# Layer 2 of a hybrid decoder step: its first seven products read the un-normed residual, and LayerNorm is spread over the chunks

## The chip, the core and the metric

The kernel runs on one core of a Trainium2 chip. The metric is the device time of one execution in microseconds. One profiled execution gives the trace that is read below. TensorE multiplies matrices (a weight load, then a matmul that streams the columns of the other operand); VectorE, ScalarE and GpSimd do elementwise work; SyncE issues most transfers.

## The reference, cut to what matters

One inference step of a two-layer trunk over 320 tokens (256 of a prompt, 8 x 8 samples) with a model width of 2048. Each layer projects `x`, runs three branches (retention, pooling, windowed attention), merges them, projects back and norms the residual:

```python
h = x @ w_in                      # 2048 -> 13824, split in qa ka va ga ub gb qc kc vc gc ma mb mc
...                               # branches a, b, c
merged = sigmoid(ma) * ya + sigmoid(mb) * yb + sigmoid(mc) * yc
y = merged @ w_out
x_new = layer_norm(alpha * x + y, ln_g, ln_b)   # (z - mean) * rsqrt(var + eps) * g + b, over 2048
```

The input of layer 2 is the `layer_norm` of layer 1's residual. Everything is float32.

## The kernel before, in words

Activations lie transposed: 16 tiles of 128 features by T = 320 tokens, four tiles in one buffer. Each float32 operand is split in a rounded high part and the rest (`h`, `l` for weights; `xh`, `xl` for the layer's input), and each 128 x 128 weight block is multiplied in three matmuls: `xh` by `h`, `xh` by `l`, `xl` by `h`.

Weights come in chunks of CH = 8 blocks (24 matmuls), 297 chunks to a layer, in the order of `layer_groups`. Layer 2 begins with a group of four products side by side (`kc` 0, `vc` 0, `qc` 0, `qc` 1; 64 blocks, 8 chunks), then `qc` 2, `qc` 3, `kc` 1, `vc` 1 and so on, two chunks each. The last products of a layer are the 16 of `wo`, each of which leaves through `done_wo`.

The program order is written by hand in `run`, and each engine works its own queue in that order. In chunk c, at position 0, `split_h(c + 2)` copies the raw weights of a chunk to their high part (ScalarE, 1024 elements a partition); at position 4, `split_l(c + 2)` subtracts that from the raw weights (VectorE), and `load(c + 6)` issues a transfer on SyncE's queue. There are three buffers for `h` and three for `l`, so the split for chunk c + 2 can't start before TensorE is done with chunk c - 1: a split is up to two chunks ahead. At the end of a chunk `pump` runs: it takes CHUNK_US = 3.26 off each engine's ledger `busy` (floor -3.0), steps the `misc` generators, and then each of three lanes (attention, two of retention) once, if the ledger of ScalarE and VectorE is under LATE_US = 1.0. The ledger is booked by `act`, `tt`, `stt`, `ts` as an instruction is issued: `tt` and `stt` book 0.15 + elements / 960 on VectorE, which is 1.22 for a weight split and 0.483 for 320 elements.

A product accumulates in PSUM: three buffers `d` (pool `psd`), five `p`. When its last matmul is issued, `done_<kind>` takes it out: `done_kc`, `done_vc`, `done_qc` copy it on ScalarE.

At the layer boundary: `done_wo(j)` adds product j to the residual z and to the running sums S and Q (of z and z squared). After j = 15 TensorE sums S and Q over features (`token_sums`), VectorE and ScalarE compute mean and inverse deviation (`norm`, first lines), TensorE spreads both over the partitions (`token_rows`), and `norm` norms the 16 tiles into new `xh`, `xl`. That part is skewed by hand:

```python
if k < 12: center(k + 4, nc.gpsimd)   # z - mean, on GpSimd
if k < 13: scaled(k + 3)              # times 1/deviation, VectorE
if k < 14: high(k + 2)                # ScalarE: times g plus b, then the copy to xh
if k:      low(k)                     # VectorE: the rest, xl
```

`need_x(k + 3)` steps it within the first group. No product of layer 2 starts before `xh` of its first tile is there.

Of the kernel before, what the change touches and what calls it, by code (L numbers as in the profile page):

```python
# [21 lines left out]
T = NP + NB * NT  # L22
PAST = 1024
# [17 lines left out]
def att_rows(t):  # L41

    p, g = divmod(t, 4)
    lo, hi = (2 * p) * 4 + g, (2 * p + 1) * 4 + g
    return np.concatenate([np.arange(lo * 64, lo * 64 + 64), np.arange(hi * 64, hi * 64 + 64)])

# [48 lines left out]
class Job:  # L95
    __slots__ = ("kind", "i", "ps", "left", "w")

    def __init__(self, kind, i):
        self.kind, self.i, self.ps, self.left = kind, i, None, n_k(kind)


class Step:
    def __init__(self, ctx, tc, io):
        self.tc, self.nc, self.io = tc, tc.nc, io
        pool = lambda n, b, **kw: ctx.enter_context(tc.tile_pool(name=n, bufs=b, **kw))
        self.cp = pool("const", 1)
        self.gp = pool("gran", 24)
        self.mp = pool("mid", 13)
        self.np = pool("mini", 6)
        self.sp = pool("small", 8)  # L110
        self.wp = pool("w", 4)
        self.hp = pool("wh", 3)
        self.lp = pool("wl", 3)
        self.pd = pool("psd", 3, space=bass.MemoryType.PSUM)
        self.pp = pool("psp", 5, space=bass.MemoryType.PSUM)
        self.raw, self.H, self.L = {}, {}, {}
        self.busy = {"a": 0.0, "v": 0.0, "p": 0.0}
        self.lanes = {"att": deque(), "ret0": deque(), "ret1": deque()}
        self.misc = []

# [161 lines left out]
    def pump(self):  # L282

        for e in self.busy:
            self.busy[e] = max(self.busy[e] - CHUNK_US, -SLACK_US)
        self.step_misc()
        for lane in self.lanes:
            if max(self.busy["a"], self.busy["v"]) < LATE_US:
                self.step(lane)
# [10 lines left out]
    def setup(self):  # L300
        nc, io = self.nc, self.io
        self.ident = self.const("ident", [128, 128])
        make_identity(nc, self.ident[:])
        self.ident_r = self.cp.tile([128, 128], F32R, tag="ident_r", name="ident_r")
        nc.vector.tensor_copy(out=self.ident_r, in_=self.ident)
        self.ones = self.const("ones", [128, 128])
        nc.vector.memset(self.ones, 1.0)
        self.ones_r = self.cp.tile([128, 128], F32R, tag="ones_r", name="ones_r")
        nc.vector.memset(self.ones_r[:].bitcast(F32), 1.0)
        yield  # L310
        self.rot = self.const("rot", [128, 2, T], io["c_rot"], nc.sync)
        self.sinkP = self.const("sinkP", [128, DEPTH, 16], io["sink_p"], nc.sync)
        self.sinkS = self.const("sinkS", [128, DEPTH, 4], io["sink_s"], nc.sync)
        self.nsinkP = self.const("nsinkP", [128, DEPTH, 16])
        self.nsinkS = self.const("nsinkS", [128, DEPTH, 4])
        yield
        yield
        self.ts(self.nsinkP, self.sinkP, -1.0)
        self.ts(self.nsinkS, self.sinkS, -1.0)
        self.dmask = self.const("dmask", [128, HA, 128], io["c_dmask"])  # L320
        self.qdec = self.const("qdec", [128, HA, 128], io["c_qdec"])
        self.maskS = self.const("maskS", [128, HA, 128], io["c_masks"])
        self.kdec = self.const("kdec", [128, HA], io["c_kdec"])
        self.kdecS = self.const("kdecS", [128, HA, NT], io["c_kdecs"])
        self.cnt = self.const("cnt", [128, 4, 16], io["c_cnt"])
        self.pscale = self.const("pscale", [128, DEPTH, 8], io["pool_scale"])
        self.lng = self.const("lng", [128, DEPTH, 16], io["ln_g"])
        self.lnb = self.const("lnb", [128, DEPTH, 16], io["ln_b"])
        self.bmask = self.const("bmask", [128, 4, 80], io["c_bmask"])
        self.flip = self.const("flip", [128, 2], io["c_flip"])  # L330
        yield
        self.biasS = self.const("biasS", [128, 4, 160], io["bias_s"])


    def run(self):
# [30 lines left out]
        for layer in range(DEPTH):  # L366
            if layer:
                self.begin_layer(layer)
            for grp in layer_groups():
                jobs = [Job(kind, i) for kind, i in grp]  # L370
                self.before(jobs[0].kind, jobs[0].i)
                for k in range(n_k(grp[0][0])):
                    if len(jobs) > 1:
                        self.need_x(min(k + 3, 15))
# [19 lines left out]
    def block(self, job, k, c, pos):  # L394
        if job.ps is None:
            if job.kind == "qc" and job.i == 1:
                job.ps = self.p([128, T])
            else:
                job.ps = self.pd.tile([128, T], F32, tag="d", name="d")
# [14 lines left out]
    def part(self, pair, k):  # L414
        return pair[0][k // 4][:, k % 4, :], pair[1][k // 4][:, k % 4, :]
# [7 lines left out]
    def rhs(self, job, k):  # L423
        kind = job.kind
        if kind in ("ya", "yb", "yc"):
            return self.part(self.gated[kind[1]], k)
# [7 lines left out]
    def begin_layer(self, l):  # L434
# [3 lines left out]
        self.x_gen = self.x_from_input() if l == 0 else self.norm(l - 1, zs, False)  # L438
# [13 lines left out]

    def x_from_input(self):
        self.x = ([], [])
        for k in range(16):
            if k % 4 == 0:
                self.x[0].append(self.g([128, 4, T], F32R, name=f"xh{k}"))
                self.x[1].append(self.g([128, 4, T], F32R, name=f"xl{k}"))
# [4 lines left out]
    def before(self, kind, i):  # L463
# [14 lines left out]
        if kind == "wo" and i == 0:  # L478
            self.z = [self.g([128, 4, T], name=f"z{n}") for n in range(4)]

# [245 lines left out]

    def done_kc(self, p, ps):
        nc, l = self.nc, self.l
        kv = self.g([128, 2, T], name="kv")
        self.copy(kv[:, 0, :], ps)  # L730
# [7 lines left out]
    def done_vc(self, p, ps):  # L738
        nc, l = self.nc, self.l
        kv = self.att[p]["kv"]  # L740
        self.copy(kv[:, 1, :], ps)
# [3 lines left out]
    def done_qc(self, t, ps):  # L745
        p, g = divmod(t, 4)
        self.copy(self.att[p]["q"][:, g, :], ps)
# [247 lines left out]
    def done_wo(self, j, ps):  # L995
# [10 lines left out]
        if j == 1:  # L1006
            self.drain("misc")
            for i in range(2):
                zi = self.z[0][:, i, :]
                self.tt(zi, zi, self.cen, ALU.subtract)  # L1010
            self.S = self.m([128, T], name="S")
# [6 lines left out]
        self.tt(self.Q, self.Q, sq, ALU.add)  # L1018
        if j < 15:
# [7 lines left out]
        if j == 15:  # L1027
            self.pS, self.pQ = self.token_sums(self.S), self.token_sums(self.Q)

# [8 lines left out]
    def norm(self, l, zs, final):  # L1038
        nc = self.nc
        st = self.s(16)  # L1040
        mu, ms, v, y, t = (st[:, 3 * i:3 * i + 3] for i in range(5))
        tile_of = lambda k: zs[k // 4][:, k % 4, :]
        M = self.m([128, T], name="M")
# [4 lines left out]
        def affine(k, out):  # L1048
            g, b = self.lng[:, l, k:k + 1], self.lnb[:, l, k:k + 1]
            self.act(out=out, in_=tile_of(k), func=AF.Identity, bias=b, scale=g)  # L1050

        def affine_v(k, out):
            self.ts(out, tile_of(k), self.lng[:, l, k:k + 1], self.lnb[:, l, k:k + 1])
# [5 lines left out]
        self.act(out=t, in_=v, func=AF.Sqrt)  # L1059
# [4 lines left out]
        if final:  # L1064
            return self.last(tile_of, center, affine, affine_v, pR)
        center(0)
        for k in range(1, 4):
            center(k, nc.gpsimd)
        self.x = ([], [])
        for k in range(4):  # L1070
            self.x[0].append(self.g([128, 4, T], F32R, name=f"xh{k}"))
            self.x[1].append(self.g([128, 4, T], F32R, name=f"xl{k}"))

        def scaled(k):
            self.tt(tile_of(k), tile_of(k), pR, ALU.mult)

        first = {}

        def high(k):
            h = self.part(self.x, k)[0]  # L1080
            if k < 2:
                affine(k, h)
                first[k] = self.m([128, T], name="x0")
                affine_v(k, first[k])
            else:
                affine(k, tile_of(k))
                self.copy(h, tile_of(k))

        def low(k):
            h, lo = self.part(self.x, k)  # L1090
            self.tt(lo, first.get(k, tile_of(k)), h.bitcast(F32), ALU.subtract)

        def rest():
            for k in range(2):
                scaled(k)
                high(k)
            low(0)
            scaled(2)
            for k in range(16):
                if k < 12:  # L1100
                    center(k + 4, nc.gpsimd)
                if k < 13:
                    scaled(k + 3)
                if k < 14:
                    high(k + 2)
                if k:
                    low(k)
                yield

        return rest()  # L1110

    def last(self, tile_of, center, affine, affine_v, pR):
        nc = self.nc
# [37 lines left out]
    def finish(self):  # L1151
        self.norm(DEPTH - 1, self.z, True)
# [141 lines left out]
```

## Time and profile before

| | |
|---|---|
| runs (us) | median 2295.2, lowest 2294.62 |
| the profiled execution | 2294.67, of which the profile's span is 2292.8 |
| mean granted TensorE clock | 0.995 |
| TensorE busy | 99% of the span |
| VectorE, ScalarE, GpSimd busy | 53%, 41%, 4% |
| layer boundary | about 1138 to 1150 us |

Times in rows are microseconds from the span's start unless marked ns. A row of the timeline gives start, length, engine, line, operation, output<-input and the idle time in front of it with what ended it. Matmuls are pipelined, so a row of 0.31 us does not mean a pace of 0.31: the pace is the distance between starts. The same holds, less strongly, for VectorE and ScalarE. Many lines are those of helpers: L176 is `act`, L183 `tt`, L187 `stt`, L197 `mm`.

### The profile page before, as it was taken

The page shows a single profiled execution, that of the slowest core. Times are in us where ns is not written, and L with a number is a line of the kernel's source. Part 1 is how long each engine was busy: PE and PEld are TensorE (multiplying, and loading weights), DVE is VectorE, ACT ScalarE, POOL GpSimd, SP SyncE. Part 2 cuts the span into 40 slices and gives each one's busy share as a digit, 9 for nine tenths or more (in the row PEclk, how much of TensorE's full clock was granted, in tenths as well). Part 3 has the DMA queues.
Part 4 walks back from the last instruction along what each step waited for, and adds up shares of the span by engine and source line. Part 5 has one row for each costly group of instructions (what it writes and reads, how often), then busy time and mean ns, then how long its engine had stood idle before and what let it go on. Part 6 is the DMA issues. An engine that isn't in the chain of part 4 may idle for free.

```text
span 2292.8 us, 37711 instructions
## 1 busy us (share of the span) xinstructions
PE 2265.2 (99%) x15660; PEld 2213.3 (97%) x15660; DVE 1207.3 (53%) x1861; ACT 944.2 (41%) x1534; POOL 99.4 (4%) x155
## 2 busy tenths in 40 slices
PE   8999999999999999999999999999999999999997
PEld 8998999999999999999998989999999999999997
DVE  4645557545444444446656455575544444454566
ACT  4545445343333343333365444443434333433333
POOL 1000000000000000000020001000000000000001
PEclk9999999999999999999999999999999999999998
DMA  7443454544444444444453435445444444444442
GB/s 271 143 148 122 151 203 150 193 147 155 148 152 151 147 148 154 150 148 149 137 193 118 138 129 188 159 162 197 148 147 152 152 148 147 156 148 147 147 149 100
DMA packets 97628, 354.92 MB, mean 155 GB/s; under 512 B 11520, under 2 KB 11968, under 8 KB 97392
## 3 DMA queue, kind: packets, MB, share of 16 engines
q1 hardware_dynamic: 93312, 335.87, 43.8%
q0 software_dynamic: 4144, 16.64, 2.0%
q8 instruction: 123, 2.02, 0.4%
q14 instruction: 49, 0.40, 0.1%
HBM read 338.51 MB, written 17.88 MB: 155 GB/s over the span
## 4 chain that ended last, share of the span: by engine, by line
PE 97%; DVE 1%; ACT 1%; DMA 1%; SPq 0%; issue 0%
PE d L197 91%; PE p L197 5%; PE p L206 1%; PE p L201 1%; DMA w<-w 1%; DVE z L183 0%; ACT acc L176 0%; DVE l L183 0%; ACT h L176 0%; ACT L176 0%; SPq L340 0%; DVE z L194 0%; ACT z L176 0%; SPq L150 0%; DVE pp L187 0%
## 5 line engine op out<-in xcount | busy, mean ns | idle before, releaser
L183 DVE TENSOR_TENSOR l<-w,h 128x1024 fp32r<-128x1024 f32 (+1 forms) x597 | 737.8, 1237 | 719.9 <-ACT h L176 719.2
L197 PE MATMUL d<-xh,h 128*128 128x320 f32 x3424 | 1071.6, 313 | 7.7 <-ACT xh L176 7.6
L197 PE MATMUL d<-xh,l 128*128 128x320 f32 x3424 | 1059.2, 310 | 1.4 <-DVE l L183 1.4
L197 PE MATMUL d<-xl,h 128*128 128x320 f32 x3424 | 1049.1, 310 | 0.0
L176 ACT ACTIVATE h<-w 128x1024 fp32r<-128x1024 f32 (+1 forms) x597 | 628.3, 1053 | 517.9 <-PE d L197 351.3
L197 PEld LDWEIGHTS d<-xh,h 128*128 128x128 f32 x3424 | 644.3, 188 | 19.8 <-ACT xh L176 8.3
L197 PEld LDWEIGHTS d<-xh,l 128*128 128x128 f32 x3424 | 644.6, 188 | 2.3 <-DVE l L183 1.9
L197 PEld LDWEIGHTS d<-xl,h 128*128 128x128 f32 x3424 | 641.5, 188 | 0.0
L197 PE MATMUL d<-mgh,h 128*128 128x320 f32 x512 | 158.7, 310 | 0.0
L197 PE MATMUL d<-mgh,l 128*128 128x320 f32 x512 | 158.2, 309 | 0.0
L197 PE MATMUL d<-mgl,h 128*128 128x320 f32 x512 | 158.2, 309 | 0.0
L197 PEld LDWEIGHTS d<-mgh,h 128*128 128x128 f32 x512 | 96.1, 188 | 0.2
L197 PEld LDWEIGHTS d<-mgh,l 128*128 128x128 f32 x512 | 96.1, 188 | 0.2
L197 PEld LDWEIGHTS d<-mgl,h 128*128 128x128 f32 x512 | 96.1, 188 | 0.0
L176 ACT ACTIVATE sig<-d 128x320 f32<-128x320 f32 x64 | 28.0, 438 | 149.7 <-PE d L197 149.7
L197 PE MATMUL d<-gbh,h 128*128 128x320 f32 x256 | 79.1, 309 | 0.0
L197 PE MATMUL d<-gbh,l 128*128 128x320 f32 x256 | 79.1, 309 | 0.0
L197 PE MATMUL d<-gbl,h 128*128 128x320 f32 x256 | 79.1, 309 | 0.0
L197 PE MATMUL d<-gah,h 128*128 128x320 f32 x256 | 79.1, 309 | 0.0
L197 PE MATMUL d<-gah,l 128*128 128x320 f32 x256 | 79.1, 309 | 0.0
L197 PE MATMUL d<-gal,h 128*128 128x320 f32 x256 | 79.1, 309 | 0.0
L197 PE MATMUL d<-gch,h 128*128 128x320 f32 x256 | 79.1, 309 | 0.0
(235 smaller groups left out, 1941.3 us busy)
## 6 DMA issues: line engine op xcount, KB each, us to landing
w<-w SPq DMA_DIRECT2D x595, 512.0 KB, 3.3
s<-s SPq DMA_DIRECT2D x16, 512.0 KB, 5.8
o_rets<-s POOLq DMA_DIRECT2D x16, 512.0 KB, 5.3
bias<-bias_p SPq DMA_DIRECT2D x8, 512.0 KB, 5.5
o_x<-z SPq DMA_DIRECT2D x8, 320.0 KB, 2.2
ck<-ck SPq DMA_DIRECT2D x4, 512.0 KB, 5.2
cv<-cv SPq DMA_DIRECT2D x4, 512.0 KB, 6.5
xin<-x SPq DMA_DIRECT2D x3, 640.0 KB, 12.5
```

Of the source, the lines that this page charges most:

```text
L176: self.nc.scalar.activation(out=out, in_=in_, func=func, **kw)
L183: (eng or self.nc.vector).tensor_tensor(out=out, in0=a, in1=b, op=op)
L197: self.nc.tensor.matmul(out, lhsT=lhsT, rhs=rhs, start=start, stop=stop)
L201: self.nc.tensor.matmul(out, lhsT=lhsT, rhs=rhs, start=False, stop=True, skip_group_check=True)
L206: self.nc.tensor.transpose(out, in_, ident[:n, :n])
```

## The change

The first seven products of layer 2 (`EARLY`: `kc` 0, `vc` 0, `qc` 0 to 3, `kc` 1; 112 blocks, 14 chunks) take as input u = z times g, the residual of layer 1 times the norm's scale, before the norm. `unnormed` writes its high and low part over the old `xh`, `xl` as each product of `wo` leaves. Two more columns (T becomes TU = 322) hold g and b, so that each of these products carries W'g and W'b with it, and `take` forms (u-product - mean x W'g) / deviation + W'b as the product leaves PSUM: ScalarE copy, VectorE `stt`, VectorE `tt`, ScalarE activation.

The norm itself becomes a generator that `pump` steps at the end of each chunk while `norming` is set: first `token_sums` and the statistics, then the two row spreads copied to SBUF as M and R, then one tile a step, at least one step a chunk and more while VectorE's ledger is under 1.0. Meanwhile the lanes are not stepped. A tile is now centred on VectorE, not GpSimd, and the skew is gone. `drain_x` finishes what is left before the first product that is not early.

```diff
+EARLY = {("kc", 0), ("vc", 0), ("qc", 0), ("qc", 1), ("qc", 2), ("qc", 3), ("kc", 1)}
...
         self.step_misc()
+        if self.norming:
+            self.step_norm()
+            return
         for lane in self.lanes:
...
                 for k in range(n_k(grp[0][0])):
-                    if len(jobs) > 1:
-                        self.need_x(min(k + 3, 15))
+                    if layer == 0:
+                        if len(jobs) > 1:
+                            self.need_x(min(k + 3, 15))
+                    elif not jobs[0].early:
+                        self.drain_x()
...
+        if job.early:
+            return tuple(t[k // 4][:, k % 4, :] for t in self.u)
...
+        if l:
+            self.u, self.norming, self.rows_done = self.x, True, False
+        self.x_gen = self.x_from_input() if l == 0 else self.norm(l - 1, zs)
...
+    def step_norm(self):
+
+        first = True
+        while self.norming and (first or self.rows_done and self.busy["v"] < LATE_US):
+            first = False
+            self.norming = next(self.x_gen, False) is None
...
+    def take(self, out, ps):
+
+        if ps.shape[1] == T:
+            self.copy(out, ps)
+            return
+        t = self.m([128, TU], name="tk")
+        self.copy(t, ps)
+        u = t[:, 0:T]
+        self.stt(u, self.M, t[:, T:T + 1], u, ALU.mult, ALU.subtract)
+        self.tt(u, u, self.R, ALU.mult)
+        self.act(out=out, in_=u, func=AF.Identity, bias=t[:, T + 1:TU], scale=-1.0)
+
     def done_kc(self, p, ps):
...
-        self.copy(kv[:, 0, :], ps)
+        self.take(kv[:, 0, :], ps)
...
+    def unnormed(self, k):
+
+        if self.l < DEPTH - 1:
+            h, lo = self.part(self.x, k)
+            z, g = self.z[k // 4][:, k % 4, :], self.lngb[:, self.l, k, 0:1]
+            self.act(out=h, in_=z, func=AF.Copy, scale=g)
+            self.stt(lo, z, g, h.bitcast(F32), ALU.mult, ALU.subtract)
...
+    def norm(self, l, zs):
+
+        tile_of = lambda k: zs[k // 4][:, k % 4, :]
+        self.pS, self.pQ = self.token_sums(self.S), self.token_sums(self.Q)
+        mu, v, y, t = self.stats()
+        self.rsqrt(y, v, t)
+        yield
+        self.M = self.m([128, T], name="M")
+        self.copy(self.M, self.token_rows(mu))
+        self.R = self.m([128, T], name="R")
+        self.copy(self.R, self.token_rows(y))
+        self.rows_done = True
+        yield
+        self.x = ([], [])
+        for k in range(16):
...
+            z = tile_of(k)
+            h, lo = self.part(self.x, k)
+            self.tt(z, z, self.M, ALU.subtract)
+            self.tt(z, z, self.R, ALU.mult)
+            self.act(out=z, in_=z, func=AF.Identity, bias=self.lngb[:, l, k, 1:2], scale=self.lngb[:, l, k, 0:1])
+            self.hl(h, lo, z)
+            yield
```

Beside this, the input buffers `xh`, `xl` of both layers are allocated 322 wide (their rows lie 1288 bytes apart instead of 1280), g and b arrive in one transfer instead of two, and the identity and the ones are kept once instead of twice. The end of the kernel (`last`) has the same order as before.

## Rows read from the trace of the kernel before

**Rows 1.** The page: engines' busy time, then the commonest matmul of three alike

```profile
PE 2265.2 (99%) x15660; PEld 2213.3 (97%) x15660; DVE 1207.3 (53%) x1861; ACT 944.2 (41%) x1534; POOL 99.4 (4%) x155
...
L197 PE MATMUL d<-xh,h 128*128 128x320 f32 x3424 | 1071.6, 313 | 7.7 <-ACT xh L176 7.6
```

**Rows 2.** TensorE's waits, whole span: us in total, times, longest

```profile
PE d L197 <- ACT xh L176: 7.6, 3, 4.5
...
PE d L197 <- DVE l L183: 1.4, 2, 0.9
```

**Rows 3.** Windows at the boundary: engines' busy us (instructions), granted clock, DMA share, GB/s

```profile
1140.00:1145.00 5.00, 3.17 (x22) 2.89 (x21) 3.89 (x14) 1.95 (x4) 3.07 (x4) 0.82 0.07 28
1145.00:1150.00 5.00, 5.00 (x20) 5.00 (x20) 5.00 (x10) 3.70 (x7) 5.00 (x6) 0.50 0.00 0
1150.00:1155.00 5.00, 5.00 (x35) 5.00 (x35) 4.45 (x8) 4.91 (x8) 5.00 (x5) 1.00 0.26 75
```

**Rows 4.** The chain that ended last: start, us, what; one chunk undisturbed

```profile
117.65 3.52 PE d L197 x24
```

**Rows 5.** Timeline of TensorE at the layer boundary

```profile
1137.68 0.31 PE L197 MATMUL d<-mgl,h 128*128 128x320 f32 x1
1139.10 0.83 PE L197 MATMUL p<-ones,S 128*128 128x1 f32 x6 [1.11 <-DVE S L183]
1139.79 0.81 PE L197 MATMUL p<-ones,Q 128*128 128x1 f32 x6
1140.46 0.86 PE L197 MATMUL p<-ident,s 128*128 128x128 f32 x6
...
1144.03 0.63 PE L197 MATMUL d<-xh,h 128*128 128x320 f32 x1 [1.27 <-ACT xh L176]
...
1150.35 0.30 PE L197 MATMUL d<-xh,h 128*128 128x320 f32 x1
```

**Rows 6.** Timeline of VectorE and ScalarE at the layer boundary

```profile
1138.03 0.49 DVE L183 TENSOR_TENSOR z<-z,d 128x320 f32<-128x320 f32 x1 [1.15 <-PE d L197]
1138.55 0.49 DVE L183 TENSOR_TENSOR S<-S,z 128x320 f32<-128x320 f32 x1
...
1141.36 0.44 ACT L176 ACTIVATE M<-p 128x320 f32<-128x320 f32 x1 [0.32 <-PE p L197]
...
1141.67 0.16 DVE L187 SCALAR_TENSOR_TENSOR s<-s 128x3 f32<-128x3 f32 x1
...
1143.71 0.47 DVE L183 TENSOR_TENSOR z<-z,p 128x320 f32<-128x320 f32 x1
...
1144.22 0.65 ACT L176 ACTIVATE xh<-z,lnb,lng 128x320 fp32r<-128x320 f32 x1 [0.24 <-DVE z L183]
```

**Rows 7.** Timeline of ScalarE while the tiles are normed, and later

```profile
1161.57 0.64 ACT L176 ACTIVATE z<-z,lnb,lng 128x320 f32<-128x320 f32 x1
1162.24 0.47 ACT L176 ACTIVATE xh<-z 128x320 fp32r<-128x320 f32 x1
1162.62 1.05 ACT L176 ACTIVATE h<-w 128x1024 fp32r<-128x1024 f32 x1
...
1171.66 1.06 ACT L176 ACTIVATE h<-w 128x1024 fp32r<-128x1024 f32 x1 [2.46 <-PE p L197]
```

**Rows 8.** Timeline of VectorE in the same stretch

```profile
1161.19 0.48 DVE L183 TENSOR_TENSOR xl<-z,xh 128x320 fp32r<-128x320 f32 x1
1161.60 1.21 DVE L183 TENSOR_TENSOR l<-w,h 128x1024 fp32r<-128x1024 f32 x1
1162.73 0.48 DVE L183 TENSOR_TENSOR z<-z,p 128x320 f32<-128x320 f32 x1
...
1172.75 1.23 DVE L183 TENSOR_TENSOR l<-w,h 128x1024 fp32r<-128x1024 f32 x1 [2.29 <-ACT h L176]
```

**Rows 9.** Timeline of TensorE in the first chunks of the kernel

```profile
18.99 0.42 PE L197 MATMUL d<-xh,l 128*128 128x320 f32 x1 [0.92 <-DVE l L183]
19.24 0.31 PE L197 MATMUL d<-xh,h 128*128 128x320 f32 x1
19.39 0.31 PE L197 MATMUL d<-xh,l 128*128 128x320 f32 x1
```

More of the change, by code (lines that the diff above doesn't have):

```diff
@@ L22 @@
 T = NP + NB * NT
+TU = T + 2
 PAST = 1024
@@ L95, with __init__ @@
 class Job:
-    __slots__ = ("kind", "i", "ps", "left", "w")
-    def __init__(self, kind, i):
+    __slots__ = ("kind", "i", "ps", "left", "w", "early")
+    def __init__(self, kind, i, layer):
         self.kind, self.i, self.ps, self.left = kind, i, None, n_k(kind)
+        self.early = layer > 0 and (kind, i) in EARLY
 class Step:
@@ L119, in __init__ @@
         self.misc = []
+        self.norming = False
     def g(self, shape, dt=F32, name="g"):
@@ L301, in setup @@
         nc, io = self.nc, self.io
-        self.ident = self.const("ident", [128, 128])
-        make_identity(nc, self.ident[:])
         self.ident_r = self.cp.tile([128, 128], F32R, tag="ident_r", name="ident_r")
-        nc.vector.tensor_copy(out=self.ident_r, in_=self.ident)
-        self.ones = self.const("ones", [128, 128])
+        self.ident = self.ident_r[:].bitcast(F32)
+        ident = self.m([128, 128], name="ident0")
+        make_identity(nc, ident[:])
+        nc.vector.tensor_copy(out=self.ident_r, in_=ident)
+        self.ones_r = self.cp.tile([128, 128], F32R, tag="ones_r", name="ones_r")
+        self.ones = self.ones_r[:].bitcast(F32)
         nc.vector.memset(self.ones, 1.0)
-        self.ones_r = self.cp.tile([128, 128], F32R, tag="ones_r", name="ones_r")
-        nc.vector.memset(self.ones_r[:].bitcast(F32), 1.0)
         yield
@@ L326, in setup @@
         self.pscale = self.const("pscale", [128, DEPTH, 8], io["pool_scale"])
-        self.lng = self.const("lng", [128, DEPTH, 16], io["ln_g"])
-        self.lnb = self.const("lnb", [128, DEPTH, 16], io["ln_b"])
+        self.lngb = self.const("lngb", [128, DEPTH, 16, 2], io["ln_gb"])
         self.bmask = self.const("bmask", [128, 4, 80], io["c_bmask"])
@@ L369, in run @@
             for grp in layer_groups():
-                jobs = [Job(kind, i) for kind, i in grp]
+                jobs = [Job(kind, i, layer) for kind, i in grp]
                 self.before(jobs[0].kind, jobs[0].i)
                 for k in range(n_k(grp[0][0])):
-                    if len(jobs) > 1:
-                        self.need_x(min(k + 3, 15))
+                    if layer == 0:
[3 more added lines that the diff above has]
+                        self.drain_x()
                     for n, job in enumerate(jobs):
@@ L395, in block @@
         if job.ps is None:
+            n = TU if job.early else T
             if job.kind == "qc" and job.i == 1:
-                job.ps = self.p([128, T])
+                job.ps = self.p([128, n])
             else:
-                job.ps = self.pd.tile([128, T], F32, tag="d", name="d")
+                job.ps = self.pd.tile([128, n], F32, tag="d", name="d")
         job.w = h, lo = self.H[c][:, pos, :], self.L[c][:, pos, :]
@@ L414, in part @@
     def part(self, pair, k):
-        return pair[0][k // 4][:, k % 4, :], pair[1][k // 4][:, k % 4, :]
+        return pair[0][k // 4][:, k % 4, 0:T], pair[1][k // 4][:, k % 4, 0:T]
     def pair(self, n, name):
@@ L437, in begin_layer @@
         self.xk = 0
-        self.x_gen = self.x_from_input() if l == 0 else self.norm(l - 1, zs, False)
+        if l:
+            self.u, self.norming, self.rows_done = self.x, True, False
+        self.x_gen = self.x_from_input() if l == 0 else self.norm(l - 1, zs)
         self.oC = [None, None]
@@ L451, in need_x, with drain_x @@
             self.xk += 1
+    def step_norm(self):
[3 more added lines that the diff above has]
+            self.norming = next(self.x_gen, False) is None
+    def drain_x(self):
+        while self.norming:
+            self.norming = next(self.x_gen, False) is None
     def x_from_input(self):
@@ L456, in x_from_input @@
             if k % 4 == 0:
-                self.x[0].append(self.g([128, 4, T], F32R, name=f"xh{k}"))
-                self.x[1].append(self.g([128, 4, T], F32R, name=f"xl{k}"))
+                self.x[0].append(self.g([128, 4, TU], F32R, name=f"xh{k}"))
+                self.x[1].append(self.g([128, 4, TU], F32R, name=f"xl{k}"))
             h, lo = self.part(self.x, k)
@@ L479, in before @@
             self.z = [self.g([128, 4, T], name=f"z{n}") for n in range(4)]
+            if self.l < DEPTH - 1:
+                for n in range(4):
+                    self.hl(
+                        self.x[0][n][:, :, T:], self.x[1][n][:, :, T:], self.lngb[:, self.l, 4 * n:4 * n + 4, :]
+                    )
     def rotary(self, ps, dst, scale):
@@ L740, in done_vc @@
         kv = self.att[p]["kv"]
-        self.copy(kv[:, 1, :], ps)
+        self.take(kv[:, 1, :], ps)
         nc.gpsimd.dma_start(out=self.io["o_wv"][l, p], in_=kv[:, 1, 128:T])
@@ L746, in done_qc @@
         p, g = divmod(t, 4)
-        self.copy(self.att[p]["q"][:, g, :], ps)
+        self.take(self.att[p]["q"][:, g, :], ps)
         if g == 3:
@@ L1010, in done_wo @@
                 self.tt(zi, zi, self.cen, ALU.subtract)
+                self.unnormed(i)
             self.S = self.m([128, T], name="S")
@@ L1018, in done_wo @@
         self.tt(self.Q, self.Q, sq, ALU.add)
+        if j > 1:
+            self.unnormed(j)
         if j < 15:
@@ L1026, in done_wo @@
             self.act(out=dummy, in_=self.ones[:, 0:1], func=AF.Sqrt)
-        if j == 15:
+        if j == 15 and self.l == DEPTH - 1:
             self.pS, self.pQ = self.token_sums(self.S), self.token_sums(self.Q)
+    def unnormed(self, k):
+        if self.l < DEPTH - 1:
+            h, lo = self.part(self.x, k)
+            z, g = self.z[k // 4][:, k % 4, :], self.lngb[:, self.l, k, 0:1]
+            self.act(out=h, in_=z, func=AF.Copy, scale=g)
+            self.stt(lo, z, g, h.bitcast(F32), ALU.mult, ALU.subtract)
     def center(self, z):
@@ L1036, in center, with stats @@
         yield
-    def norm(self, l, zs, final):
-        nc = self.nc
+    def stats(self):
         st = self.s(16)
         mu, ms, v, y, t = (st[:, 3 * i:3 * i + 3] for i in range(5))
-        tile_of = lambda k: zs[k // 4][:, k % 4, :]
-        M = self.m([128, T], name="M")
-        def center(k, eng=None):
-            self.tt(tile_of(k), tile_of(k), M if eng else pM, ALU.subtract, eng)
[L1048 to L1053, printed above, removed]
         self.ts(mu, self.pS, 1.0 / D)
@@ L1059, in norm, with last, center, affine @@
         self.act(out=t, in_=v, func=AF.Sqrt)
+        return mu, v, y, t
+    def norm(self, l, zs):
[12 more added lines that the diff above has]
+        for k in range(16):
+            if k % 4 == 0:
+                self.x[0].append(self.g([128, 4, T], F32R, name=f"xh{k}"))
+                self.x[1].append(self.g([128, 4, T], F32R, name=f"xl{k}"))
+            z = tile_of(k)
[5 more added lines that the diff above has]
+            yield
+    def last(self):
+        nc, l = self.nc, DEPTH - 1
+        tile_of = lambda k: self.z[k // 4][:, k % 4, :]
+        M = self.m([128, T], name="M")
+        def center(k, eng=None):
+            self.tt(tile_of(k), tile_of(k), M if eng else pM, ALU.subtract, eng)
+        def affine(k, out):
+            g, b = self.lngb[:, l, k, 0:1], self.lngb[:, l, k, 1:2]
+            self.act(out=out, in_=tile_of(k), func=AF.Identity, bias=b, scale=g)
+        def affine_v(k, out):
+            self.ts(out, tile_of(k), self.lngb[:, l, k, 0:1], self.lngb[:, l, k, 1:2])
+        mu, v, y, t = self.stats()
         pM = self.token_rows(mu)
@@ L1063, in norm @@
         pR = self.token_rows(y)
[L1064 to L1113, printed above, removed]
         R = self.m([128, T], name="R")
@@ L1151, in finish @@
     def finish(self):
-        self.norm(DEPTH - 1, self.z, True)
+        self.last()
 def constants():
@@ L1258 @@
         pool_scale=perkt(a["pool_scale"], 8),
-        ln_g=perkt(a["ln_g"], 16),
-        ln_b=perkt(a["ln_b"], 16),
+        ln_gb=np.stack([perkt(a["ln_g"], 16), perkt(a["ln_b"], 16)], axis=3),
         **bias_tables(a["rel_bias"]),
```

## The prediction

> **What bounds the kernel now.** I read the busy line of the page first. TensorE is at work for 99% of the span, VectorE for 53% and ScalarE for 41% [rows 1]. So the time is the length of TensorE's stream, 24 matmuls (one chunk of eight weight blocks) in 3.52 us [rows 4], plus whatever interrupts it. The view of TensorE's waits says how little does: all its waits for an operand come to some 12 us in 2292.8, and the largest, 7.6 us, is for `xh`, the split input of a layer [rows 2]. [...] The last matmul of layer 1 starts at 1137.68, so its successor could start at 1137.83. Layer 2's first matmul starts at 1144.03, behind a chain of token sums, statistics and two row spreads. That is 6.2 us lost. The 24 matmuls from 1144.03 to 1150.35 take 6.32 us where 3.52 is the usual: another 2.8 us at the lower clock. The boundary costs 9.0 us, 0.4% of the time, and this change can win no more than that.
>
> **What goes away.** Layer 2's first seven products (14 chunks) read the un-normed residual, which is ready before the boundary, so TensorE runs straight on: 9.0 us won. I charge three small items against it. Token sums and row spreads no longer lie in a bubble but in the stream: four groups at about 0.68 us (1139.10 to 1139.79 to 1140.46 [rows 5]), 2.7 us. The third product needs the PSUM buffer that `z` of the last product leaves at 1138.03 + 0.49 [rows 6], against 1137.83 + 4 x 0.147 = 1138.42: 0.1 us. Two more columns in 336 matmuls at 0.147/320 us a column: 0.3 us. Left: 5.9 us. The extra `unnormed` in each output product (one ScalarE, one VectorE instruction of about 0.5 us per two chunks) costs nothing: VectorE has idle time in each chunk there (1.15 us in front of `z` alone [rows 6]), and with that cover gone it would only delay the next `z` by 0.5 us. The set-up edits (one DMA fewer, a shared `ones`) lie under the first loads: nothing either way.
>
> **What is added, and where it lies.** In the kernel before, the norm is written skewed: `scaled(k+3)`, `high(k+2)`, `low(k)`, so VectorE always has a neighbour's work while ScalarE scales a tile. In the new `norm` each tile is one unbroken chain: VectorE subtract, VectorE multiply, ScalarE affine, ScalarE copy, VectorE subtract. VectorE takes its queue in order, so the next tile starts behind the last subtract. From rows: a VectorE result to a VectorE reader 0.52 us (1138.03 to 1138.55); VectorE to ScalarE 0.51 (1143.71 to 1144.22) [rows 6]; affine to its copy 0.67 (1161.57 to 1162.24 [rows 7]); copy to VectorE 0.50 (0.47 long, and 0.03 as from the end of `h` at 1172.72 [rows 7] to `l` at 1172.75 [rows 8]); to the next tile's subtract 0.41 (1161.19 to 1161.60 [rows 8]). Sum: **2.61 us a tile**, of which VectorE works about 1.4.
>
> In the same two queues stand the weight splits, one `h` (ScalarE) and one `l` (VectorE) for each chunk. The code issues, chunk by chunk, `h`, `l`, then the tiles. So `h` waits behind the last tile's copy and `l` behind `h`: copy to `h` 0.38 (1162.24 to 1162.62), `h` 1.06 + 0.03, `l` to the next subtract 1.13 (1161.60 to 1162.73), less the 0.91 already in the tile: **1.68 us more for each chunk** [rows 7, 8]. A chunk with one tile takes 4.29 us, with two 6.90, and TensorE eats one in 3.52.
>
> How many tiles are issued per chunk follows from the ledger `busy["v"]`. Layer 2 begins at its floor, -3.0. A chunk adds 1.22 (its `l`) and takes off 3.26; a tile adds 3 x 0.483 = 1.45; a `take` adds 0.97; tiles are issued while the ledger is under 1.0, and always one. After chunk 1 come the statistics, after chunk 2 the rows and tiles until -3.0 + 3 x 1.45 = 1.35. Carried on, chunks 2 to 13 issue 3, 2, 1, 1, 2, 1, 1, 1, 1, 1, 1, 1 tiles: 16. The ledger sees 1.45 where the queue takes 2.61, so it can't see the lag.
>
> The walk. Chunk 1 starts at 1137.83; chunk 3 at 1137.83 + 2 x 3.52 + 2.8 (with the small groups) = 1147.7. The spread of `mu` starts at 1146.3, that of `y` 0.67 later, and their ScalarE copies begin 0.90 behind (1140.46 to 1141.36 [rows 5, 6]) and take 0.44, so the first multiply can start at 1148.38 and its tile counts from 1147.86. `y` itself is ready: 2.0 us from the sums of Q (1139.79 to 1141.67 + 0.16 [rows 5, 6]), a whole chunk ahead. Third tile's copy: 1147.86 + 2 x 2.61 + 1.70 = 1154.8. Then `h` and `l` of chunk 5: 0.38 + 1.06 + 0.03 + 1.22 = 2.7, ready at 1157.5. TensorE wants them at 1147.7 + 2 x 3.52 = 1154.7. **From chunk 5 on it is late**, by 2.7 us, and from here each chunk is paid in full by the two queues.
>
> The takes come at the end of chunks 8 (four of them), 10, 12 and 14. One is ScalarE copy, VectorE, VectorE, ScalarE, some 2.17 us by the same rows. The first copy runs under the `l` in front of it, so the four add 3 x 2.17 + 0.92 = 7.4 and each later one 0.92 us (its two VectorE operations). The first of the four also holds the PSUM buffer that the next product wants, so TensorE stands still there for some 7 us and again for 5 us two chunks later; these are parts of the lag, not on top.
>
> Ready for chunk 16: 1147.86 + 15 x 2.61 + 1.70 + 11 x 1.68 + 7.4 + 2 x 0.92 + 2.7 = 1219.1. In the kernel before, chunk 16 starts at 1144.03 + 2.8 + 15 x 3.52 = 1199.6 (work of the attention lane in between left out on both sides, it is the same). So TensorE is 19.5 us behind the old kernel: 5.9 won, 25.4 stalled. The last `take` still delays chunk 17 by about 0.5. Then the tiles are out, and the queues need 2.3 us a chunk. The attention lane, which waits for the end of the norm, starts with no lead of splits in hand: between 0 and 4 us, I take 1, since `pump` gives it work only under the same ledger. Sum: **+21 us**, from 2294.67 (the profiled execution, 1.9 over its span, between the lowest, 2294.62, and the median, 2295.2, of the runs): 2315.7. I say 2315.
>
> **A cost the trace doesn't show.** Rows of `xh` and `xl` become 322 elements, 1288 bytes apart, where 1280 was a multiple of 256. No matmul of the kernel before reads such rows. Below it is nothing, and a gain is excluded, since no fewer columns are read; above I take one more column for each of the 3 x 3424 matmuls [rows 1], 0.46 ns each, 4.7 us. I take 0, as the copies already in the page keep their pace at odd offsets in the same memory, and keep 4.7 for the range. [...]
>
> **The rivals.**
> *The splits arrive in time (0.12).* If a tile cost only VectorE's own pace, three times 0.41, the chain would keep up. The point where this decides: TensorE needs 13 chunks, 45.8 us, from chunk 3 to chunk 16, and the splits have a lead of 7.04 - 2.3 = 4.7 us, so 16 tiles may cost 50.5 - 12 x 1.68 - 9.2 = 21 us, 1.3 each. For it: the ledger assumes it, and the old kernel's VectorE kept such a pace [rows 8]. Against it: that pace belongs to the skewed order. Then the 5.9 us are won whole: 2294.67 - 5.9, about 2289, faster than before.
> *Part of the lag is hidden (0.08).* Were the takes or the `h` behind a tile less in the way than in the walk (half of 9.2 and of 12 x 1.68), 15 us fall away: about 2300.
> *The clock falls in the stalls (0.07).* [...] Against it: after a wait of 0.92 us for `l` the next starts (19.24, 19.39) are at full pace again [rows 9], and a slow chunk mostly fills a later wait. Full price 3 x 2.8 = 8.4: 2324.
> *Longer rows cost a column (0.05).* 4.7 us: 2320.
>
> **How the numbers follow.** The walk holds with 0.68. Its own range is 2308 to 2322: 0.1 us on a tile is 1.6, the takes may be 3 less, attention 0 to 4, rows 0 to 4.7. Adding the near side of the hidden lag and of the slow clock gives 2299 to 2324 for 8 times in 10. Two per cent is 46 us, about what a measurement of this kernel can tell from no change. The boundary has 9 us to give, so faster by over 2%: 0.01. Slower needs twice my lag, which only slow clock, rows and a long attention backlog together would bring: 0.03. Within: 0.96.
>
> **What would show it.** The boundary without a gap and at clock 1.00 between 1138 and 1154. In TensorE's waits, `d` on VectorE `l` and ScalarE `h` with some 20 us in all, where `l` now has 1.4 [rows 2], and one wait for `kv`'s copy at the end of chunk 8. VectorE rows with idle time behind ScalarE `z` and `xh` in each tile, tiles 2.6 us apart. I am wrong if TensorE waits less than 5 us between 1150 and 1225, or if its pitch of 0.147 has changed.

## The result, and the profile after

The changed kernel takes 2321.18 us (2319.52 to 2321.65) against 2295.2: a ratio of 1.0113, with an interval of 1.0102 to 1.0124. It is 26 us slower, inside the range of 2299 to 2324 and within 2%, and 6 us above the 2315 that were named.

In the changed file the helpers stand seven lines lower: L183 is now `act`, L190 `tt`, L194 `stt`, L204 `mm`. The page's span and busy lines:

```profile
span 2319.9 us, 37765 instructions
...
PE 2279.4 (98%) x15660; PEld 2224.7 (96%) x15660; DVE 1228.2 (53%) x1907; ACT 960.8 (41%) x1566; POOL 83.7 (4%) x139
```

TensorE issues as many instructions as before [rows 1], and is at work for 14 us longer in a span that is 27 us longer. First the boundary, in the timeline of TensorE:

```profile
1144.92 0.31 PE L204 MATMUL d<-mgl,h 128*128 128x320 f32 x1
1145.06 0.31 PE L204 MATMUL d<-xh,h 128*128 128x322 f32 x1
```

The first product of layer 2 follows the last of layer 1 at the usual distance; the 6.2 us of [rows 5] are gone. But the last matmul of layer 1 starts at 1144.92 where it was 1137.68: 7.2 us are lost before the boundary is reached. The windows behind it (engines' busy time and counts, granted clock, DMA share, GB/s) answer to [rows 3]:

```profile
1140.00:1150.00 10.00, 10.00 (x71) 9.74 (x70) 7.02 (x12) 4.92 (x7) 0.00 (x0) 1.00 0.34 110
1150.00:1160.00 10.00, 10.00 (x73) 10.00 (x73) 4.59 (x12) 4.24 (x8) 0.00 (x0) 1.00 0.31 103
1160.00:1170.00 10.00, 7.78 (x40) 7.17 (x39) 5.70 (x11) 4.71 (x9) 0.00 (x0) 0.83 0.17 52
1170.00:1180.00 10.00, 8.09 (x50) 7.26 (x49) 6.11 (x10) 4.76 (x7) 0.00 (x0) 1.00 0.31 107
1180.00:1190.00 10.00, 3.74 (x24) 3.40 (x23) 5.77 (x11) 4.71 (x8) 0.00 (x0) 0.95 0.31 99
1190.00:1200.00 10.00, 9.07 (x46) 9.07 (x47) 6.32 (x12) 4.11 (x9) 1.17 (x2) 0.71 0.51 184
1200.00:1210.00 10.00, 7.42 (x31) 6.93 (x30) 6.19 (x11) 5.34 (x9) 0.00 (x0) 0.66 0.28 86
```

At the boundary the clock stays at 1.00 and TensorE has no gap. From 1160 on it stands, up to 6.3 us in ten, while VectorE and ScalarE are busy for only 41 to 63% of the time: neither is full, both wait for each other. TensorE's waits from 1130 to 1260 (us in total, times, longest), to be set against [rows 2]:

```profile
PE d L204 <- ACT tk L183: 6.7, 1, 6.7
PE d L204 <- DVE l L190: 5.4, 8, 0.8
PE d L204 <- ACT h L183: 4.0, 4, 1.7
```

All three are what the prediction's walk through the chunks named: a PSUM buffer behind the first `take`, and the two halves of the weights. The chain that holds them up, one chunk with one tile, in the timeline of VectorE and then of ScalarE:

```profile
1170.63 1.23 DVE L190 TENSOR_TENSOR l<-w,h 128x1024 fp32r<-128x1024 f32 x1 [0.45 <-ACT h L183]
1171.78 0.48 DVE L190 TENSOR_TENSOR z<-z,M 128x320 f32<-128x320 f32 x1
1172.30 0.49 DVE L190 TENSOR_TENSOR z<-z,R 128x320 f32<-128x320 f32 x1
1174.01 0.49 DVE L190 TENSOR_TENSOR xl<-z,xh 128x320 fp32r<-128x320 f32 x1 [1.23 <-ACT xh L183]
1174.96 1.23 DVE L190 TENSOR_TENSOR l<-w,h 128x1024 fp32r<-128x1024 f32 x1 [0.46 <-ACT h L183]
```

```profile
1172.82 0.65 ACT L183 ACTIVATE z<-z,lngb 128x320 f32<-128x320 f32 x1 [2.22 <-DVE z L190]
1173.51 0.47 ACT L183 ACTIVATE xh<-z 128x320 fp32r<-128x320 f32 x1
1173.89 1.04 ACT L183 ACTIVATE h<-w 128x1024 fp32r<-128x1024 f32 x1
```

From `l` to `l` it is 4.33 us, where 4.29 were predicted and TensorE needs 3.52. VectorE idles 1.23 us behind `xh` and 0.46 behind `h`; ScalarE idles 2.22 behind `z`. Between two tiles of the same chunk it is 2.64 us from subtract to subtract, where 2.61 were predicted:

```profile
1157.84 0.48 DVE L190 TENSOR_TENSOR z<-z,M 128x320 f32<-128x320 f32 x1
...
1160.48 0.48 DVE L190 TENSOR_TENSOR z<-z,M 128x320 f32<-128x320 f32 x1
```

Now the start of the same weight matmul in both kernels. The changed kernel is 0.3 us late at the 50th, 7.2 us at the end of layer 1, 1.25 us at chunk 4 of layer 2, when the boundary's gain is in, 25.8 us at chunk 16, when the chain lets go, and 26.7 us at the end. (Between chunk 16 and about chunk 60 the attention lane's work lies at other places in the two kernels, so single starts can't be compared there.) So there are two losses, 6.9 us in layer 1 and 25.4 us behind the boundary, around one gain of 6.0 us.

Of the 6.9 us in layer 1, 0.6 come at one place, the start of the fourth output product (1053 us), where an `l` comes late. The first two `unnormed` stand one behind the other on VectorE, each waiting for ScalarE's `xh`, and the splits for the next chunks stand behind them:

```profile
1047.81 0.55 DVE L194 SCALAR_TENSOR_TENSOR xl<-z,lngb,xh 128x320 fp32r<-128x320 f32 x1 [0.63 <-ACT xh L183]
...
1049.40 0.55 DVE L194 SCALAR_TENSOR_TENSOR xl<-z,lngb,xh 128x320 fp32r<-128x320 f32 x1 [0.63 <-ACT xh L183]
```

### The profile page after: what moved, and what is told of

Read it like the earlier page. It is cut to its first block, busy times and chain, and to the rows that moved or that the text cites. A ratio compares the mean times of both kernels' runs of the same rounds, so it can differ in the third digit from the quotient of the medians.

```text
span 2319.9 us, 37765 instructions
## 1 busy us (share of the span) xinstructions
PE 2279.4 (98%) x15660; PEld 2224.7 (96%) x15660; DVE 1228.2 (53%) x1907; ACT 960.8 (41%) x1566; POOL 83.7 (4%) x139
## 4 chain that ended last, share of the span: by engine, by line
PE 95%; DVE 2%; ACT 2%; DMA 0%; issue 0%; SPq 0%; ACTq 0%; DVEq 0%
PE d L204 88%; PE p L204 4%; PE p L213 1%; DVE z L190 1%; PE p L208 1%; DVE l L190 1%; ACT h L183 1%; ACT z L183 1%; DMA w<-w 0%; ACT xh L183 0%; DVE tk L194 0%; DVE tk L190 0%; ACT acc L183 0%; DVE xl L190 0%; DVE z L201 0%
## 5 line engine op out<-in xcount | busy, mean ns | idle before, releaser
L190 DVE TENSOR_TENSOR l<-w,h 128x1024 fp32r<-128x1024 f32 (+1 forms) x597 | 736.6, 1235 | 697.9 <-ACT h L183 697.3
L204 PE MATMUL d<-xh,h 128*128 128x320 f32 (+1 forms) x3424 | 1074.7, 314 | 18.3 <-ACT xh L183 7.5
L204 PE MATMUL d<-xh,l 128*128 128x320 f32 (+1 forms) x3424 | 1063.9, 311 | 5.9 <-DVE l L190 5.9
L204 PE MATMUL d<-xl,h 128*128 128x320 f32 (+1 forms) x3424 | 1050.6, 310 | 0.0
L183 ACT ACTIVATE h<-w 128x1024 fp32r<-128x1024 f32 (+1 forms) x597 | 628.1, 1053 | 499.2 <-PE d L204 345.7
L204 PEld LDWEIGHTS d<-xh,h 128*128 128x128 f32 x3424 | 646.9, 189 | 30.7 <-ACT xh L183 8.0
L204 PEld LDWEIGHTS d<-xh,l 128*128 128x128 f32 x3424 | 646.9, 189 | 8.5 <-DVE l L190 8.2
L204 PEld LDWEIGHTS d<-xl,h 128*128 128x128 f32 x3424 | 645.2, 189 | 0.0
L204 PE MATMUL d<-mgh,h 128*128 128x320 f32 x512 | 159.0, 310 | 0.0
L204 PE MATMUL d<-mgl,h 128*128 128x320 f32 x512 | 158.8, 310 | 0.0
L204 PE MATMUL d<-mgh,l 128*128 128x320 f32 x512 | 158.1, 309 | 0.3 <-DVE l L190 0.3
L204 PEld LDWEIGHTS d<-mgh,l 128*128 128x128 f32 x512 | 96.4, 188 | 0.7 <-DVE l L190 0.6
L204 PEld LDWEIGHTS d<-mgl,h 128*128 128x128 f32 x512 | 96.3, 188 | 0.0
L204 PEld LDWEIGHTS d<-mgh,h 128*128 128x128 f32 x512 | 96.2, 188 | 0.2
L183 ACT ACTIVATE sig<-d 128x320 f32<-128x320 f32 x64 | 28.0, 438 | 149.8 <-PE d L204 149.8
L204 PE MATMUL d<-gcl,h 128*128 128x320 f32 x256 | 79.2, 310 | 0.0
L204 PE MATMUL d<-gbl,h 128*128 128x320 f32 x256 | 79.2, 309 | 0.0
L204 PE MATMUL d<-gbh,h 128*128 128x320 f32 x256 | 79.1, 309 | 0.0
L204 PE MATMUL d<-gch,h 128*128 128x320 f32 x256 | 79.1, 309 | 0.0
L204 PE MATMUL d<-gal,h 128*128 128x320 f32 x256 | 79.1, 309 | 0.0
L204 PE MATMUL d<-gch,l 128*128 128x320 f32 x256 | 79.0, 309 | 0.0
L204 PE MATMUL d<-gbh,l 128*128 128x320 f32 x256 | 79.0, 309 | 0.0
```

The lines of the kernel that those rows point to most:

```text
L183: self.nc.scalar.activation(out=out, in_=in_, func=func, **kw)
L190: (eng or self.nc.vector).tensor_tensor(out=out, in0=a, in1=b, op=op)
L204: self.nc.tensor.matmul(out, lhsT=lhsT, rhs=rhs, start=start, stop=stop)
```

## Experiments

**The rows of layer 1, put into the kernel before.** Its own norm and order stay.

```diff
     def x_from_input(self):
...
-                self.x[0].append(self.g([128, 4, T], F32R, name=f"xh{k}"))
+                self.x[0].append(self.g([128, 4, T + 2], F32R, name=f"xh{k}"))
...                                        # xl alike; part() takes [.., 0:T]
```

> The kernel before, with the input buffers of layer 1 alone allocated 322 wide (rows 1288 bytes apart, buffers of 5152 bytes); the identity and the ones are kept once, to make room. Nothing of the norm or its order changes. If the longer rows slow the matmuls that read them (147.7 ns a matmul on average in the changed kernel's layer 1, 146.67 in the kernel before), layer 1 becomes 5 to 7.5 us longer and the time is 2300 to 2303 us, with layer 2 as before. If layer 1's loss in the changed kernel comes from the extra work of unnormed or from the start of the kernel, the time is 2294 to 2296.

Measured: 2301.83 us against 2294.34, ratio 1.0032 (1.0019 to 1.0046). The rows, in buffers of this size, cost 7.5 us alone.

**The same buffers with the old rows.** Buffers of 4 x 320 + 8 elements, viewed as four rows of 320.

```diff
-                self.x[0].append(self.g([128, 4, T], F32R, name=f"xh{k}"))
+                self.x[0].append(self.g([128, 4 * T + 8], F32R, name=f"xh{k}")[:, 0:4 * T]
+                                 .rearrange("p (n t) -> p n t", n=4))
```

> As the last, with the same buffers of 5152 bytes, so that every second buffer begins at 32 bytes past a multiple of 64, but with the rows inside them 1280 bytes apart as before. If the distance of the rows is the cause: 2294 to 2297 us. If the start addresses of the buffers are: 2299 to 2303, and the pitch of gated products is off 146.67 too.

Measured: 2295.81 us, ratio 1.0007 (0.9997 to 1.0017). The interval includes no change: where these buffers begin hardly matters, the distance of the rows inside them does. (With the distance, the start of each row within its buffer changes too; no run parts the two.) By starts, this run and the one before both lose 1.3 to 1.8 us in layer 2, whose rows are 320 in both, so some 6 of the 7.5 us are the longer rows'.

**Rows of 1312 bytes in the changed kernel.**

```diff
+TR = T + 8
...
-                self.x[0].append(self.g([128, 4, TU], F32R, name=f"xh{k}"))
+                self.x[0].append(self.g([128, 4, TR], F32R, name=f"xh{k}"))
...                                        # xl alike; the early products read [.., 0:TU]
-        self.mp = pool("mid", 13)
+        self.mp = pool("mid", 12)
```

> The changed kernel with the input rows of layer 1 at 328 elements, 1312 bytes (a multiple of 32) in place of 1288 (a multiple of 8), and one middle-sized buffer fewer to make room. If rows that start off a multiple of 32 are what costs 7 us in layer 1: 2313 to 2315 us. If anything off a multiple of 64 costs as much, it stays at 2319 to 2322.

Measured: 2313.72 us, ratio 1.0083 (1.0068 to 1.0098): 7.5 us back. One undisturbed stretch of layer 1, 4392 matmuls in the chain that ended last (start, us, what), is in turn that of the kernel before, of the kernel before with rows of 322 (and its layer 2, where rows are 320 again), of the one with 5152-byte buffers, of the changed kernel with 1312-byte rows, and of the changed kernel itself:

```profile
391.11 644.27 PE d L197 x4392
```

```profile
392.70 647.71 PE d L197 x4392
...
1532.54 644.97 PE d L197 x4392
```

```profile
390.87 644.41 PE d L197 x4392
```

```profile
390.71 644.48 PE d L205 x4392
```

```profile
393.98 647.71 PE d L204 x4392
```

Only the 1288-byte rows make the stretch longer, by 3.4 us. From each start to the next, the matmuls that read these rows in layer 1 have a mean pitch of 147.8 ns in the changed kernel, in place of 146.6 in the kernel before. By place in the buffer, over the 3130 such matmuls of the stretch, it is 146.8, 148.2, 147.1 and 149.0, where the kernel before has 146.7 at each place. With 1312-byte rows the stretch is 0.2 us longer than in the kernel before, under 0.1 ns for each of the 3130.

**Without the correction in `take`.** The early products leave by one copy.

```diff
-        if ps.shape[1] == T:
-            self.copy(out, ps)
+        if True:
+            self.copy(out, ps[:, 0:T])
             return
```

> The changed kernel without the correction in take: the early products leave by one ScalarE copy as in the kernel before, so layer 2's first seven products stay un-normed. If the walk's price of the takes is right (7.4 us for the four, 0.9 for each later one, all of it in TensorE's stall), the time falls by 8 to 9.5 us, to 2311 to 2313. If the takes lie beside other work, it stays at 2319 to 2321.

Measured: 2316.21 us, 5.0 less than the changed kernel, where 8 to 9.5 were expected. TensorE's longest wait is as long as before, now for the plain copy, so it is the queue in front of that copy and not the correction that holds the PSUM buffer:

```profile
PE d L204 <- ACT kv L183: 6.7, 1, 6.7
```

The trace shows why this was no clean removal: without the takes' bookings the ledger is lower, two tiles instead of one are issued at the ends of chunks 8 and 10, and the norm ends two chunks earlier. By the walk TensorE then had 2 x (3.52 - 1.68) = 3.7 us less of its own work to set against the chain, and 9.2 - 3.7 = 5.5 is what was seen within 0.5. So the ledger was held:

```diff
             self.copy(out, ps[:, 0:T])
+            if ps.shape[1] != T:
+                self.busy["v"] += 2 * (0.15 + T / 960.0)
             return
```

> The changed kernel without the correction in take (layer 2's first seven products stay un-normed), but with the 0.967 that a take books in VectorE's ledger still booked, so that the tiles stay at the chunks where they are in the changed kernel. If the walk's price of the takes holds for a fixed order: 2311 to 2313 us. If it was too high and not the tiles' moving up made the last run without takes fall by 5 only: 2316.

Measured: 2312.04 us, 9.1 less. With the order held the takes cost what the walk said.

**The norm's skew put back.** One group of lines moved, no instruction more or fewer. What a step books moves with it, so the later chunks with two tiles are 5 and 7 in place of 3 and 6; the norm ends at the same chunk.

```diff
+            for n in ((0, 1) if k == 0 else (k + 1,)):
+                if n < 16:
+                    self.tt(tile_of(n), tile_of(n), self.M, ALU.subtract)
+                    self.tt(tile_of(n), tile_of(n), self.R, ALU.mult)
             z = tile_of(k)
             h, lo = self.part(self.x, k)
-            self.tt(z, z, self.M, ALU.subtract)
-            self.tt(z, z, self.R, ALU.mult)
             self.act(out=z, in_=z, func=AF.Identity, bias=..., scale=...)
             self.hl(h, lo, z)
```

> The changed kernel with one thing moved: a step of the norm issues subtract and multiply of the next tile before the affine, copy and last subtract of this one, so that VectorE has work while ScalarE scales. As many instructions on each engine as in the changed kernel, the same ledger, the same tiles per chunk. If the unbroken chain of 2.61 us a tile is what starves TensorE, a tile costs some 1.4 us, the waits for h and l before the takes vanish, the four takes still cost about 5 us of stall, and the time is 2298 to 2305 us. If the amount of VectorE work is what starves TensorE (rival): 2318 to 2322.

Measured: 2302.73 us, ratio 1.0033 (1.0021 to 1.0045), 18.5 less than the changed kernel. A chunk with one tile, VectorE of this kernel:

```profile
1161.76 1.22 DVE L190 TENSOR_TENSOR l<-w,h 128x1024 fp32r<-128x1024 f32 x1
1162.89 0.48 DVE L190 TENSOR_TENSOR z<-z,M 128x320 f32<-128x320 f32 x1
1163.41 0.49 DVE L190 TENSOR_TENSOR z<-z,R 128x320 f32<-128x320 f32 x1
1163.82 0.48 DVE L190 TENSOR_TENSOR xl<-z,xh 128x320 fp32r<-128x320 f32 x1
1164.22 1.22 DVE L190 TENSOR_TENSOR l<-w,h 128x1024 fp32r<-128x1024 f32 x1
```

The same instructions take 2.46 us from `l` to `l` instead of 4.33, with no wait inside. The amount of VectorE work was not the bound; the order was. TensorE's waits in this stretch fall to 5.0 us: 3.4 for `h` and 0.8 for `l` after the four takes, 0.8 for the PSUM buffer.

**Skew, and the takes put off.** `take` copies PSUM at once and leaves `stt`, `tt` and the activation to the next ends of chunks, one product each.

```diff
         self.copy(t, ps)
-        u = t[:, 0:T]
-        self.stt(u, self.M, t[:, T:T + 1], u, ALU.mult, ALU.subtract)
-        self.tt(u, u, self.R, ALU.mult)
-        self.act(out=out, in_=u, func=AF.Identity, bias=t[:, T + 1:TU], scale=-1.0)
+        self.late.append((out, t, then))
...
+        late = bool(self.late)
+        if late:
+            self.step_late()               # those three, and the transfer that reads them
         if self.norming:
             self.step_norm()
+        if late or self.norming:
             return
```

> As the last, and the takes are split too: the ScalarE copy out of PSUM at once, the other three instructions (and the transfer of k or v that reads them) one product a chunk at the next ends of chunks. If the takes' chain was the rest of the stall, TensorE runs on through the first 17 chunks: 2294.7 - 5.9 + 7.3 for layer 1's longer rows = 2296, 2294 to 2298 us. If the rest has another cause, it stays where the run with the skew alone is.

Measured: 2301.13 us, ratio 1.0027 (1.0017 to 1.0037). That missed: hardly better than the skew alone.

**Skew, late takes and rows of 1312 bytes.** The last kernel with the edit of the rows from above:

```diff
+TR = T + 8
...
-                self.x[0].append(self.g([128, 4, TU], F32R, name=f"xh{k}"))
+                self.x[0].append(self.g([128, 4, TR], F32R, name=f"xh{k}"))
```

> As the last, with layer 1's input rows 1312 bytes apart in place of 1288. If the three causes add up, the boundary's gain is left alone: 2288 to 2291 us, 0.1 to 0.3% under the kernel before. If clock or lanes take it back: 2293 or more.

Measured: 2294.01 us, ratio 0.9997 (0.9988 to 1.0005). The rows' 7 us came back again, but 5 us of the boundary's gain were still missing. VectorE in a chunk of this kernel:

```profile
1184.98 1.23 DVE L192 TENSOR_TENSOR l<-w,h 128x1024 fp32r<-128x1024 f32 x1 [0.46 <-ACT h L185]
1186.12 0.55 DVE L196 SCALAR_TENSOR_TENSOR tk<-M,tk 128x320 f32<-128x320 f32 x1
1186.70 0.49 DVE L192 TENSOR_TENSOR tk<-tk,R 128x320 f32<-128x320 f32 x1
1187.11 0.48 DVE L192 TENSOR_TENSOR z<-z,M 128x320 f32<-128x320 f32 x1
1187.63 0.49 DVE L192 TENSOR_TENSOR z<-z,R 128x320 f32<-128x320 f32 x1
1188.87 0.49 DVE L192 TENSOR_TENSOR xl<-z,xh 128x320 fp32r<-128x320 f32 x1 [0.75 <-ACT xh L185]
1189.82 1.22 DVE L192 TENSOR_TENSOR l<-w,h 128x1024 fp32r<-128x1024 f32 x1 [0.46 <-ACT h L185]
```

Again 4.84 us from `l` to `l`, for the same reason as in the changed kernel: ScalarE's half of the take waits for VectorE's, and the tile's `xh` and the next `h` stand behind it. Putting the takes off had moved the chain, not cut it.

**The takes in two halves.** VectorE's half after the chunk's tile, ScalarE's half at the end of the next chunk. A first form, which held the lanes back one chunk longer, deadlocked and has no time; why is not shown.

```diff
-        late = bool(self.late)
-        if late:
-            self.step_late()
+        if self.part2:
+            self.late_a()                  # activation of the take before, and its transfer
         if self.norming:
             self.step_norm()
-        if late or self.norming:
+        if self.late:
+            self.late_v()                  # stt and tt of the next take
+        if self.norming or len(self.late) + bool(self.part2) > 1:
             return
```

> The run with skew, late takes and rows of 1312 bytes, its takes parted further: the VectorE half of a take is issued after the chunk's tile, its ScalarE half at the end of the next chunk, so that ScalarE never waits for VectorE inside a chunk; the lanes start again one chunk earlier. In the run before it a chunk with a tile and a late take took 4.84 us (l to l), because h stood behind the take's ScalarE half and that behind its VectorE half. By the same rows a chunk now needs 1.13 + 0.52 + 0.41 + 0.41 + 0.58 + 0.41 = 3.46 us of VectorE and 2.5 of ScalarE, under TensorE's 3.52: no wait for l between the boundary and chunk 17, and 2288 to 2290 us. If the 5 us come from something else than that order (lanes that start late, the clock), it stays at 2293 to 2295.

Measured: 2289.39 us, ratio 0.9978 (0.9968 to 0.9988): the boundary's gain is left, and this is faster than both kernels. The chunk is now 3.46 us, and TensorE's only wait from 1125 to 1260 is the last line:

```profile
1173.33 1.22 DVE L192 TENSOR_TENSOR l<-w,h 128x1024 fp32r<-128x1024 f32 x1
1174.47 0.49 DVE L192 TENSOR_TENSOR z<-z,M 128x320 f32<-128x320 f32 x1
1174.99 0.49 DVE L192 TENSOR_TENSOR z<-z,R 128x320 f32<-128x320 f32 x1
1175.40 0.48 DVE L192 TENSOR_TENSOR xl<-z,xh 128x320 fp32r<-128x320 f32 x1
1175.80 0.55 DVE L196 SCALAR_TENSOR_TENSOR tk<-M,tk 128x320 f32<-128x320 f32 x1
1176.38 0.49 DVE L192 TENSOR_TENSOR tk<-tk,R 128x320 f32<-128x320 f32 x1
1176.79 1.22 DVE L192 TENSOR_TENSOR l<-w,h 128x1024 fp32r<-128x1024 f32 x1
...
PE d L206 <- ACT tk L185: 0.7, 1, 0.7
```

## Why the prediction was right, and where it was off

*The boundary's gain* was 5.9 us in the sum, out of 6.2 us of waiting [rows 5] and 2.8 us of matmuls at the granted clock of [rows 3]. By the starts of the same matmul it is 6.0 us (from 7.2 late to 1.25), and the last run, in which little is left of the losses, is 5.3 us under the kernel before.

*The chain of 2.61 us a tile and 1.68 a chunk* was right: 4.33 us a chunk measured for 4.29, and 2.64 a tile. By chunk 16 the first chunks of layer 2 lost 24.6 us (25.8 - 1.25) where the walk had 25.4. That the order and not the work is the cause is shown by the skew alone, which adds and removes no instruction.

*The takes* were priced at 9.2 us and cost 9.1 with the order held. That they also set the ledger, so that removing them moves tiles, was not in the walk.

*The last take and the attention lane* were taken at +0.5 and +1 us. Together they are 0.9 (25.8 to 26.7 late); no run parts them.

*The step that failed is the term for the longer rows.* The prediction took 0 and bounded it by 4.7 us, one column for each of 3 x 3424 matmuls. Both numbers were off, and so was a reading: the text ahead speaks of the input buffers of both layers, but the new `norm` allocates layer 2's at 320, so only layer 1's half of these matmuls reads such rows, and of layer 2's only the early products. Layer 1 loses 6.9 us, of which 0.6 are not the rows' (next paragraph). The other 6.3 are 1.2 ns a matmul, by which the pitch rose too, where the bound was 0.46; 0.3 of them lie in the output products, which don't read these rows, and the run with the old rows in 5152-byte buffers has the same 0.3 there. The bound was a guess, since no row of the kernel before could show such a matmul, and the argument that copies keep their pace at odd offsets said nothing of TensorE: in the kernel before, ScalarE's copies of 128 x 256 elements to `ext`, which start at its byte 60, take 385 ns, and its other instructions of that size out of PSUM 369 to 386. The rival "Longer rows cost a column", with a chance of 0.05 and 2320 us, is the one that came true, at a higher price; by the prediction's own sign, a changed pitch, this term was wrong.

*The term for `unnormed`* was nothing, because VectorE has idle time in each chunk. It was 0.6 us: the idle time is there, but the first two `unnormed` are a chain across two engines in front of an `l`. Every traced kernel with the change has this step of 0.5 to 0.6 us, and the kernel before with the longer rows alone has none.

With 6.9 in place of 0 for layer 1, 24.6 in place of 25.4 for the chain, and 0.9 in place of 1.5 behind it, the sum gives 2315.7 + 6.9 - 0.8 - 0.6 = 2321.2, against 2321.2 measured.

What in the distance of the rows slows a matmul is not shown. The changed kernel takes 2321.2 us with rows 1288 bytes apart and 2313.7 with rows 1312 bytes apart. By place, the second and the fourth row of a buffer are the slow ones (148.2 and 149.0 ns, against 146.8 and 147.1); but if the pitch is charged to the matmul behind it, the third and the fourth are, so the places settle nothing. Both distances that cost little here, 1280 and 1312 bytes, are multiples of 32, and 1288 is a multiple of 8; no other distance was run.

*The rival of the falling clock* came true without its price. From 1160 to 1210 us the windows show granted clocks of 0.83, 1.00, 0.95, 0.71 and 0.66. The 3 in its price of 3 x 2.8 was the author's estimate: no run shows which stalls lower the clock. The listed waits are 16 us, and those for the two halves of the weights only 9.4 where some 20 were forecast; yet the lag is nearly that of the walk. So slow matmuls seem to have filled time in which TensorE would have waited, and the clock to have cost nothing by itself here. That is argued from the windows and the lag, and no run took the clock's share apart.

## What to carry to other kernels

When an engine's queue is written in order, price a step by its chain across engines, not by the work it books: with three short VectorE operations around two ScalarE ones in a row, a chunk of one tile took 4.33 us, and 2.46 with the tiles skewed by one; a ledger that counts work can't see the difference. A step put off is only cheaper if no engine waits inside it (4.84 us a chunk with such waits here, 3.46 without): issue each engine's half where its input is already there. And when a buffer grows by two columns, every matmul that reads it may pay for the new distance of its rows: 1288 bytes cost 1.2 ns each here, 1312 less than 0.1. Measure it, or keep to a distance that has been measured.

## What the runs showed of the hardware that I had not expected

In the trace of the changed kernel, layer 1's matmuls whose moving operand's rows lie 1288 bytes apart have a mean pitch of 147.8 ns, although each row is read contiguously; in that of the kernel before, with 1280 bytes, it is 146.6. One stretch of 4392 matmuls takes 647.71 us at 1288 bytes, 644.27 at 1280 and 644.48 at 1312. With rows 1280 bytes apart, buffers of 5152 bytes in place of 5120 cost at most 0.2% (1.0007, up to 1.0017).
